# A hybrid decoder step on one core: r tiles 3 to 6 and two gate tiles as seven products of quarters, parked attention outputs, rooms chosen by time

## The chip, the cores and the metric

The kernel runs on one core of a Trainium2 chip. The metric is the device time of one execution in microseconds (us). A core has engines that run beside each other, each through its own instructions in order: TensorE for matrix products (PE in the profile, with its weight loads as PEld), VectorE (DVE), ScalarE (ACT), GpSimd (POOL) and SyncE (SP), which here issues most DMAs. Products land in PSUM, in banks of 512 fp32 numbers for each of the 128 partitions; everything else lies in SBUF.

## The reference

One layer of a decoder for 512 prompt tokens, 16 meta tokens ahead of them and 32 new tokens (8 running sequences of 4), all in fp32:

```python
h = x + 0.5 * rms_norm(swiglu(rms_norm(x, ffn1_pre_g), ...), ffn1_post_g)   # d_model 1024, d_ff 2816
u = rms_norm(h, mix_pre_g)
q_a, k_a, v_a, gk_low, r_a, q_b, k_b, v_b, gate_a, gate_b = split(u @ w_in)
o_a = gla(q_a, k_a, v_a, log_sigmoid(gk_low @ w_gk2 + b_gk) / 16)           # gated linear attention, 4 heads
o_a = rms_norm(o_a, gla_norm_g) * silu(r_a)
o_b = stick_breaking_attention(q_b, keys, values, sb_bias)                  # 16 heads; 256 cached rows for the running ones
m = sigmoid(gate_a) * (o_a @ w_o_gla) + sigmoid(gate_b) * (o_b @ w_o_sb)
h = h + rms_norm(m @ w_out, mix_post_g)
y = h + 0.5 * rms_norm(swiglu(rms_norm(h, ffn2_pre_g), ...), ffn2_post_g)
```

r_a, gate_a and gate_b are 1024 wide: eight tiles of 128 columns each. They are called r tiles, a tiles and b tiles below; "o tiles" are the eight tiles of `o_a @ w_o_gla`, "p tiles" those of `o_b @ w_o_sb`.

## The kernel before

Activations stand transposed (features on the partitions, up to 560 tokens along the row). Each fp32 factor is cut into a rounded part `hi` and a remainder `lo`, and a product is made of three: hi·hi, hi·lo and lo·hi. A tile of 128 output columns is made by `tile_steps`: eight **steps**, one for each 128 rows of the contraction, of six matmuls each (two halves of the tokens, 280 and 264 wide, by three products). `later(n, f)` puts `f` off by n steps; `when(n, f)` and `then(n, f)` put it at a step of a stage. The order of PE, DVE, ACT and GpSimd is the order in which these calls are made; SP's order is left to the framework.

**Seven products.** Two neighbouring tiles can be made together by `seven_steps`: the token columns, the contraction and the output columns are each cut in two, and seven products of quarters (272 wide, four matrix rows of blocks each) replace eight. That takes 14 steps of six matmuls instead of 16. It needs sums of quarters of the weights (`weight_sums`, four DVE operations for each pair), their hi and lo parts (`parts_of` on ACT, `parted_lo` on DVE, four of each), and sums of quarters of u. The latter are made once (`u_sums`), parked in DRAM (`sums_dram`), and read back later (`sums_back`, `sums_hi`, `sums_lo`). The seven products end in four PSUM banks, which five additions on DVE and three copies or activations on ACT put together.

**The stages.** FFN 1; the heads of linear attention, whose outputs `oa` stay in SBUF; eight attention pairs (`Pair`, 24 steps each, "pair 1" to "pair 8" being `pr` 0 to 7); then `pr` 8, in which the last pair's work ends beside r tiles 0 to 2 (24 steps); then the **mixer**, whose order is the list `MIXER`: "R" is a tile by `tile_steps`, "S" a pair by seven products. Before, that is r 3 to 7, o 0 to 7, a 0 and a 1 as R, then seven S pairs (b 0, a 2, b 2, a 4, b 4, a 6, b 6) with the p tiles between them. The first three S pairs stand side by side. After the mixer come `w_out` and FFN 2. Beside the r and o tiles, PE also does the running sequences' attention over the cache: `sample_keys` turns pages of keys (L2118), `sample_products` (L2132) gives logits, `sample_values` (L2218) weighs pages of values. Pages are gathered from DRAM by DMAs of GpSimd (L2069), into rooms that pass round in a list, `ring`.

**Weights** come by `fetch` (L186, or L621 for an S pair), into a ring of three buffers `raw`; a fetch waits until the oldest is free, that is until its `lo` part is made. An S pair's second buffer is asked for when the pair before it has made its first `lo`, five steps ahead of that pair's start, and is first read by `weight_sums` ten steps ahead of its own.

**Rooms.** SBUF tiles of varying life are taken from `Arena`: 150 units of 280 numbers, before in 25 rooms of six units. A room whose type changes (float32 or its rounded form) becomes a new tile, and its first writer waits for every earlier use of the room. `take` prefers the room that was given back longest ago, counted in gives.

## Time and profile before

| what | value |
|---|---|
| median of 3 runs | 1506.17 us (1505.92 to 1508.09) |
| profiled execution | 1508.72 us; span from first to last instruction 1507.0 us |
| granted TensorE clock | 0.999 |
| PE busy, weight loads busy | 1494.2 us, 1442.1 us |
| DVE busy, ACT busy, POOL busy | 1090.0 us, 771.5 us, 149.3 us |
| DMA | 180.40 MB, mean 120 GB/s |

The profiled execution lies 2.55 us above the median, 1.7 us of its time outside the span. Matmuls are pipelined, so the duration of one in the profile is longer than the time until the next one starts; what PE costs is read from starts.

### The profile page before, as it was taken

What the parts mean: (1) busy time and instruction counts of PE and PEld (TensorE: products, weight loads), DVE (VectorE), ACT (ScalarE), POOL (GpSimd) and SP (SyncE); (2) the same over time, 40 slices, a digit from 0 to 9 for tenths busy, and PEclk for the clock granted to TensorE, in tenths of its full rate; (3) what the DMA queues carried; (4) which work ended last, traced back from release to release, by engine and by line L of the source; (5) the groups of instructions that cost most, each with busy time, mean ns of one, the idle gap of its engine ahead of it and who ended that gap; (6) DMA issues with size and microseconds to landing.
All of it is one profiled execution on the core that took longest, in us unless ns stands there. A gap on an engine that the chain in (4) does not pass through costs nothing.

```text
span 1507.0 us, 29698 instructions
## 1 busy us (share of the span) xinstructions
PE 1494.2 (99%) x11941; PEld 1442.1 (96%) x11941; DVE 1090.0 (72%) x1939; ACT 771.5 (51%) x1422; POOL 149.3 (10%) x216
## 2 busy tenths in 40 slices
PE   9999999999999999999999999999999999999998
PEld 8999999999999889999888899999999999999998
DVE  5888888853787866877776534977567898888544
ACT  6545454533655556565555343634564555455334
POOL 2000000000000011123324551000000000000000
PEclk9999999999999999999999999999999999999999
DMA  8123333336565473335555568335532233333352
GB/s 250 55 86 99 99 98 97 88 101 195 147 160 148 122 112 85 91 82 118 131 105 139 169 204 192 105 96 144 152 103 79 85 111 99 99 99 89 86 168 98
DMA packets 276458, 180.40 MB, mean 120 GB/s; under 512 B 10154, under 2 KB 260736, under 8 KB 276320
## 3 DMA queue, kind: packets, MB, share of 16 engines
q1 hardware_dynamic: 270864, 161.64, 40.6%
q0 software_dynamic: 5440, 16.85, 3.2%
q8 instruction: 94, 1.54, 0.4%
q14 instruction: 44, 0.36, 0.1%
q10 hardware_dynamic: 16, 0.00, 0.0%
HBM read 155.72 MB, written 22.74 MB: 118 GB/s over the span
## 4 chain that ended last, share of the span: by engine, by line
PE 94%; DVE 2%; DMA 2%; ACT 1%; issue 0%; DVEq 0%; SPq 0%; ACTq 0%
PE acc L682 8%; PE acc L1248 8%; PE acc L1249 8%; PE acc L685 8%; PE acc L683 8%; PE acc L1250 8%; PE acc L695 7%; PE acc L698 7%; PE acc L696 7%; PE acc L1191 2%; PE acc L1188 2%; PE acc L1189 2%; PE acc L1028 1%; PE acc L1029 1%; PE acc L1030 1%; PE ps L2023 1%
## 5 line engine op out<-in xcount | busy, mean ns | idle before, releaser
L153 DVE TENSOR_TENSOR lo<-raw,hi 128x1024 fp32r<-128x1024 f32 (+1 forms) x213 | 254.9, 1197 | 125.9 <-ACT hi L661 102.5
L153 DVE TENSOR_TENSOR room<-room,room 128x544 f32<-128x544 f32 (+17 forms) x413 | 259.0, 649 | 81.4 <-ACT room L740 15.0
L682 PE MATMUL acc<-room,hi 128*128 128x280 f32 (+1 forms) x928 | 271.2, 309 | 0.2 <-DVE room L156 0.2
L1249 PE MATMUL acc<-room,hi 128*128 128x280 f32 (+1 forms) x896 | 259.3, 289 | 0.0
L1248 PE MATMUL acc<-room,hi 128*128 128x280 f32 (+1 forms) x896 | 259.3, 289 | 0.0
L1250 PE MATMUL acc<-room,lo 128*128 128x280 f32 (+1 forms) x896 | 259.1, 289 | 0.0
L683 PE MATMUL acc<-room,hi 128*128 128x280 f32 (+1 forms) x928 | 250.3, 289 | 0.1
L685 PE MATMUL acc<-room,lo 128*128 128x280 f32 (+1 forms) x928 | 192.8, 289 | 0.0
L682 PEld LDWEIGHTS acc<-room,hi 128*128 128x128 f32 x928 | 174.7, 188 | 13.1 <-issue 11.0
L683 PEld LDWEIGHTS acc<-room,hi 128*128 128x128 f32 x928 | 175.0, 189 | 2.8 <-issue 1.9
L1248 PEld LDWEIGHTS acc<-room,hi 128*128 128x128 f32 x896 | 168.6, 188 | 0.0
L1250 PEld LDWEIGHTS acc<-room,lo 128*128 128x128 f32 x896 | 168.6, 188 | 0.0
L1249 PEld LDWEIGHTS acc<-room,hi 128*128 128x128 f32 x896 | 168.4, 188 | 0.0
L959 ACT CAST hi<-raw 128x1024 fp32r<-128x1024 f32 x92 | 96.4, 1052 | 133.1 <-PE acc L1249 48.8
L661 ACT CAST hi<-raw 128x1024 fp32r<-128x1024 f32 (+1 forms) x121 | 122.7, 1015 | 72.0 <-DMA raw<-in_ffn_w_down_dram 18.6
L685 PEld LDWEIGHTS acc<-room,lo 128*128 128x128 f32 x928 | 145.0, 188 | 0.0
L695 PE MATMUL acc<-room,hi 128*128 128x280 f32 (+2 forms) x498 | 143.7, 296 | 0.9 <-ACT hi L661 0.9
L696 PE MATMUL acc<-room,hi 128*128 128x280 f32 (+2 forms) x498 | 141.5, 292 | 0.0
L698 PE MATMUL acc<-room,lo 128*128 128x280 f32 (+2 forms) x498 | 128.4, 292 | 0.7 <-DVE lo L153 0.7
L959 ACT CAST hi<-room 128x1024 fp32r<-128x1024 f32 x84 | 70.2, 836 | 80.8 <-PE acc L1249 60.3
L695 PE MATMUL acc<-room,room 128*128 128x280 f32 (+3 forms) x366 | 107.8, 295 | 0.0
L153 DVE TENSOR_TENSOR lo<-room,hi 128x1024 fp32r<-128x1024 f32 x84 | 80.2, 955 | 36.7 <-ACT hi L959 36.5
(406 smaller groups left out, 3299.5 us busy)
## 6 DMA issues: line engine op xcount, KB each, us to landing
raw<-in_w_in_dram SPq DMA_DIRECT2D x49, 512.0 KB
raw<-in_ffn_w_down_dram SPq DMA_DIRECT2D x40, 448.0 KB
raw<-in_ffn_w_gate_dram SPq DMA_DIRECT2D x64, 256.0 KB
raw<-in_ffn_w_up_dram SPq DMA_DIRECT2D x64, 256.0 KB
out_dram<-room SPq DMA_DIRECT2D x36, 256.0 KB
raw<-in_ffn_w_down_dram SPq DMA_DIRECT2D x14, 512.0 KB
raw<-in_w_in_dram SPq DMA_DIRECT2D x28, 256.0 KB
h_dram<-room SPq DMA_DIRECT2D x24, 280.0 KB
```

The costliest lines, as they stand in the source:

```text
L153: (eng or V).tensor_tensor(out=out, in0=a, in1=b, op=op)
L661: S.copy(h_, src)
L682: T.matmul(acc[h][:, : wid[h]], hi[k], a[h][0], start=(k == 0), stop=False)
L683: T.matmul(acc[h][:, : wid[h]], hi[k], a[h][1], start=False, stop=False)
L685: T.matmul(acc[h][:, : wid[h]], lo[k], a[h][0], start=False, stop=(k == KD - 1))
L695: T.matmul(acc[h][:nw, : wid[h]], wh, a[h][0], start=(k == 0), stop=False)
L696: T.matmul(acc[h][:nw, : wid[h]], wh, a[h][1], start=False, stop=False)
L698: T.matmul(acc[h][:nw, : wid[h]], wl, a[h][0], start=False, stop=(k == kt - 1))
L959: S.copy(hi[:, :kt], src)
L1248: T.matmul(x[:, :QW], hi, act[k][0], start=(first and k == 0), stop=False, skip_group_check=True)
L1249: T.matmul(x[:, :QW], hi, act[k][1], start=False, stop=False, skip_group_check=True)
L1250: T.matmul(x[:, :QW], lo, act[k][0], start=False, stop=(k == 3), skip_group_check=True)
```

## The change

- r tiles 3 and 4, 5 and 6, and a tiles 0 and 1 become S pairs. r 7 moves ahead of r 3. The a and b pairs stand between o tiles and p tiles in another order. The mixer's list now begins in `pr` 8.
- The sums of u are read back from pair 6 on (`SUMS_BACK` counts steps from the end of `pr` 8) instead of during the o tiles, and stay in SBUF from there.
- The outputs of linear attention are written to DRAM when they are made (`oa_dram`), given back, and read again by `oa_back` beside their r tile.
- The second halves of four of u's tiles are given back after r 7 (`halved`).
- Pages take rooms from the arena one by one, with no ring; the last three of the asks for value pages come 16 steps later.
- `Arena`: 20 rooms of six units and 15 of two; `take` compares times in steps, avoids what was given back within 12 steps, and opens an empty long room for a small tile only when others are worse.
- Sixteen small copies of the samples' outputs go from DVE to ACT; the first o tile reads its eight inputs in another order.

The diff, cut:

```diff
-KEEP = 5
-SUMS_BACK = (80, 88, 96, 104)
-MIXER = [("R", "r", n) for n in range(3, 8)]
-MIXER += [("R", "o", n) for n in range(8)] + [("R", "a", 0), ("R", "a", 1), ("S", "b", 0), ("S", "a", 2), ("S", "b", 2), ("R", "p", 0), ("R", "p", 1)]
-MIXER += [("S", "a", 4), ("R", "p", 2), ("R", "p", 3), ("S", "b", 4), ("S", "a", 6), ("R", "p", 4), ("R", "p", 5), ("S", "b", 6)]
-MIXER += [("R", "p", 6), ("R", "p", 7)]
+SUMS_BACK = (-85, -61, -37, -20)
+MIXER = [("R", "r", 0), ("R", "r", 1), ("R", "r", 2), ("R", "r", 7), ("S", "r", 3), ("S", "r", 5)]
+MIXER += [("R", "o", n) for n in range(4)] + [("S", "a", 0), ("R", "o", 4), ("R", "o", 5), ("S", "a", 2), ("R", "o", 6), ("R", "o", 7)]
+MIXER += [("S", "b", 0), ("S", "a", 4), ("R", "p", 0), ("R", "p", 1), ("S", "b", 2), ("R", "p", 2), ("R", "p", 3), ("S", "a", 6), ("S", "b", 4)]
+MIXER += [("R", "p", 4), ("R", "p", 5), ("S", "b", 6), ("R", "p", 6), ("R", "p", 7)]
-SPREAD = 15
-UNITS = 150
+UNITS, LONGS = 150, 20
...
-                since = max(f) if not empty else max(free) + SPREAD
+                other = empty and self.tile[c] is not None and self.tile[c].dtype != dt
+                since = max(free) if other else max(f)
                 waste = k % 2 == 0 and s % 2
                 alone = k == 1 and free[s ^ 1] is not None
-                key = (empty and empties <= self.keep, waste, tight and sum(x is not None for x in free), alone, since)
+                opens = empty and long and k <= self.SHORT
+                key = (opens and spare <= self.RESERVE, waste, self.now - since < self.RECENT, opens, alone, since)
...
+                for e in range(2):
+                    later(1, lambda e=e: nc.sync.dma_start(oa_dram[2 * hd + e], oa[hd, e]))
+                    later(6, lambda e=e: give(oa.pop((hd, e))))
...
-    def tile_steps(act, w1):
+    def tile_steps(act, w1, order=range(KD)):
...
     def page(src, i, c):
-        t = ring.pop(0)
+        t = take(512)
...
-                V.tensor_copy(ob[pr][r_, NP : NP + NS].rearrange("p (b t) -> p b t", t=4),
+                S.copy(ob[pr][r_, NP : NP + NS].rearrange("p (b t) -> p b t", t=4),
...
+    def oa_back(n):
+        o = take(NW)
+        nc.sync.dma_start(o, oa_dram[n])
+        return o
...
+    def r_pair(n):
+
+        o, t, sg, outs = {}, {}, {}, {}
+        q0, q1 = slice(0, QW), slice(QW, NW)
+
+        def load():
+            for i in range(2):
+                o[i] = oa_back(n + i)
+
+        def second():
+            t[1] = take(NW)
+            outs.update(c12=t[1][:, q0], c22=t[1][:, q1])
+
+        def first():
+            t[0] = take(NW)
+            outs.update(c11=lambda a: S.copy(t[0][:, q0], a), c21=t[0][:, q1])
+
+        def by_t(i):
+            sg[i] = take(NW)
+            S.activation(sg[i], t[i], AF.Sigmoid)
+            tt(o[i], o[i], t[i], ALU.mult)
+
+        def by_sg(i):
+            tt(o[i], o[i], sg[i], ALU.mult)
+            give(t[i], sg[i])
+            split(oas, n + i, o[i], oap)
+
+        for d, f in ((6, load), (10, second), (11, first), (14, lambda: by_t(1)), (15, lambda: by_sg(1)), (16, lambda: by_t(0)),
+                     (17, lambda: by_sg(0))):
+            later(d, f)
+        yield from seven_steps(("r", n), usum, QW, outs)
...
     def out_a(n):
-        acc = yield from tile_steps(oas, W1)
+        acc = yield from tile_steps(oas, W1, (0, 1, 2, 7, 3, 4, 6, 5) if n == 0 else range(KD))
...
+            if kind == "S":
+                weights_at(when, n, (what, t))
+            elif i > 1:
+                when(n - 5, st.split)
+                when(n - 4, st.fetch)
+            n += 14 if kind == "S" else 8
...
+            for m in range(2):
+                when(SUMS_BACK[i] + 6 + 4 * m, sums_hi, i, m)
+                when(SUMS_BACK[i] + 8 + 4 * m, sums_lo, i, m)
...
+        when(starts["r", 3], halved)
...
-            when(starts["b", 0] + 2 + 4 * i, lambda i=i: split(obs, i, ob[i], obp))
+            when(118 + 4 * i, lambda i=i: split(obs, i, ob[i], obp))
...
-            when(starts["a", 0] + 2 + i, ob_back, i)
+            when(102 + i, ob_back, i)
```

In the new list r 3 starts at step 8 of the mixer, r 5 at 22, o 0 at 36, a 0 at 68, b 0 at 128 and a 4 at 142; the mixer ends at step 276, before at 282.

More of the change, by code (lines that the diff above doesn't have):

```diff
@@ L69, in take @@
         best = None
-        empties = sum(None not in f for f in self.freed)
+        spare = sum(None not in f for f in self.freed if len(f) == self.LONG)
         for c, free in enumerate(self.freed):
-            empty = None not in free
+            empty, long = None not in free, len(free) == self.LONG
             if not empty and self.tile[c].dtype != dt:
                 continue
-            for s in range(self.CHUNK - k + 1):
+            for s in range(len(free) - k + 1):
                 f = free[s : s + k]
@@ L1444, in hybrid_step @@
     st.todo += [(win, 0, KD, c + P * pr, P, False) for pr in range(8) for c in (C_QB, C_KB, C_VB)]
-    st.todo += [(win, 0, KD, C_RA + P * n, P, False) for n in range(8)]
     def gate_weights(c):
@@ L2415, in hybrid_step @@
                 then(23, now.scan, 0, 3)
-            for n in FE:
+            for n in FE if now else ():
                 then(n, st.split, 0)
@@ L2445, in hybrid_step @@
                 then(SUM[1], last.meta_summed)
-            if pr == 4:
-                ring += [take(512) for _ in range(4)]
             if pr > 4:
@@ L2496, in hybrid_step @@
                 when(8 * i + 1, use_values, c, b0)
-            when(8 * i + 7, ask)
+        for i in range(3, 12):
+            when(8 * i - 17 if i < 8 else 8 * i - 1, ask)
         w1 = Weights(1)
```

136 lines of the change are left out of this document (64 added, 72 removed).

## The prediction

> **What bounds the kernel now.** First the page: its span, the busy line, and the sliced line of PE, DVE and the granted clock.
>
> ```profile
> span 1507.0 us, 29698 instructions
> PE 1494.2 (99%) x11941; PEld 1442.1 (96%) x11941; DVE 1090.0 (72%) x1939; ACT 771.5 (51%) x1422; POOL 149.3 (10%) x216
> PE   9999999999999999999999999999999999999998
> DVE  5888888853787866877776534977567898888544
> PEclk9999999999999999999999999999999999999999
> ```
>
> PE has work in every slice, at full clock; DVE is the second engine, and the slices with 3 and 4 (from 20 on) are the r and o tiles. A busy PE need not be a full one, so next the list of waits of PE (engine, line, waited for: us in total, times, longest).
>
> ```profile
> PE ps L2218 <- issue: 2.7, 5, 0.8
> PE acc L1476 <- DVE own L256: 1.1, 1, 1.1
> PE acc L695 <- ACT hi L661: 0.9, 1, 0.9
> ...
> PE ps L855 <- DVE room L153: 0.2, 1, 0.2
> ```
>
> The ten rows of the list come to 7.3 us in 1507. So the time is the number of matmuls times their spacing, and a change is worth what it takes off PE's stream, less the waits that it makes. For the spacing I read the timeline of PE in the mixer (start, duration, what).
>
> ```profile
> 949.75 0.29 PE L1028 MATMUL acc<-room,hi 128*128 128x272 f32 x1
> ...
> 960.58 0.29 PE L1028 MATMUL acc<-room,hi 128*128 128x272 f32 x1
> ...
> 970.05 0.40 PE L1028 MATMUL acc<-room,hi 128*128 128x272 f32 x1 [0.28 <-DVE room L153]
> ...
> 971.66 0.29 PE L1028 MATMUL acc<-room,hi 128*128 128x272 f32 x1
> ...
> 982.20 0.29 PE L682 MATMUL acc<-room,hi 128*128 128x280 f32 x1
> ...
> 994.27 0.29 PE L1028 MATMUL acc<-room,hi 128*128 128x272 f32 x1
> 994.40 0.29 PE L1029 MATMUL acc<-room,hi 128*128 128x272 f32 x1
> ...
> 1004.82 0.29 PE L682 MATMUL acc<-room,hi 128*128 128x280 f32 x1
> ```
>
> p 0 and p 1, two R tiles, run from 982.20 to 994.27: 12.07 us. The S pair behind them runs to 1004.82: 10.55 us. The three S pairs ahead (949.75, 960.58, 971.66, 982.20) took 10.83, 11.08 and 10.54 us: 0.81 us of loss together, in the first two.
>
> **PE's stream.** Three pairs of tiles (r 3 and 4, r 5 and 6, a 0 and 1) turn from R into S. Each saves 12.07 - 10.55 = 1.52 us, together 4.56 us: twelve matmuls of 96 in each pair, 36 in all. All other PE work stays, the samples' turns and products included; it is only moved against the tiles. This is the whole gain that I can count.
>
> [...]
>
> **DVE in the r tiles.** An S pair asks more of DVE than two R tiles. The rows by shape, from the mixer's stretch 949 to 1072, and the engines' busy time by stretch (us, then PE, PEld, DVE, ACT, POOL busy, clock, DMA share, GB/s):
>
> ```profile
> L153 DVE TENSOR_TENSOR lo<-raw,hi 128x1024 fp32r<-128x1024 f32 x21 | 25.6, 1221 | 3.9 <-ACT hi L661 3.0 <-ACT hi L959 0.6
> L153 DVE TENSOR_TENSOR room<-room,acc 128x272 f32<-128x272 f32 x28 | 11.9, 434 | 10.3 <-PE acc L1030 10.3
> L153 DVE TENSOR_TENSOR room<-room,room 128x544 fp32r<-128x544 f32 x15 | 10.8, 719 | 2.2 <-ACT room L2519 2.2
> L153 DVE TENSOR_TENSOR room<-room,room 128x544 f32<-128x544 f32 x12 | 8.4, 720 | 0.1
> L153 DVE TENSOR_TENSOR room<-raw,raw 128x512 f32<-128x512 f32 x12 | 8.3, 688 | 0.5 <-DMA raw<-in_w_in_dram 0.4
> L153 DVE TENSOR_TENSOR room<-acc,room 128x280 f32<-128x280 f32 x7 | 3.1, 450 | 7.7 <-PE acc L685 7.6
> ```
>
> ```profile
> 707.00:738.00 31.00, 31.00 (x244) 27.77 (x243) 22.91 (x52) 18.11 (x36) 10.61 (x12) 1.00 0.42 112
> 829.78:874.00 44.22, 42.91 (x415) 40.20 (x414) 21.73 (x51) 16.94 (x31) 24.45 (x25) 1.00 0.55 169
> 949.70:960.50 10.80, 10.77 (x86) 10.55 (x85) 10.61 (x20) 6.93 (x12) 0.00 (x0) 1.00 0.28 77
> 960.50:971.60 11.10, 10.82 (x86) 10.60 (x86) 10.45 (x17) 7.89 (x13) 0.00 (x0) 1.00 0.38 96
> 994.20:1004.80 10.60, 10.60 (x86) 10.60 (x86) 6.96 (x11) 4.90 (x8) 0.00 (x0) 1.00 0.26 64
> ```
>
> An r pair: 4 sums of weights at 0.69, lo parts 3 at 1.22 and one at 0.69, 5 additions at 0.43, 4 products at 0.72, 2 lo parts of the result at 0.72: 13.6 us. An r tile as R: 1.22, two reads of the bank at up to 0.45, a product and a lo part at 0.72: 3.6 us. Two pairs for four tiles: 27.2 - 14.2 = 13.0 us more. The stretch 829.78 to 874, r 3 to r 7 and what lies beside them, holds 21.73 us of DVE in 44.22; it becomes 34.7 us in 44.2 - 4 x 0.754 = 41.2 us, 84% (0.754 us is a step, 12.07 / 16). The rows put that between the pair at 10.61 of 10.80 (98%, 0.28 lost) and the one at 6.96 of 10.60 (66%, nothing lost). So DVE still fits, with its slack mostly used.
>
> What gets late first is the second of two S pairs side by side. The chain of waits shows it in the run of three (start, us, what):
>
> ```profile
> 957.50 1.42 DVE room L153 x3
> 958.99 0.98 issue
> 959.97 0.45 DVE room L153
> 960.50 8.01 DMA raw<-in_w_in_dram
> ...
> 969.21 0.79 DVE room L153 x2
> 970.05 0.40 PE acc L1028
> ```
>
> The second weight buffer took 8.01 us from there; it is asked for five steps ahead of one pair and first read ten steps ahead of the next, nine steps or 9 x 0.754 = 6.8 us apart; DVE then hands the last part over 0.28 us late, at 970.05. The new list has such neighbours at r 3/r 5, b 0/a 4 and a 6/b 4. The first has the samples' PE work between ask and read, which gives the DMA time, but more DVE work; the second is like 949.75 to 971.66. I take 0.81 us again, as before, and bounds of 0 to 3 x 0.53 = 1.6 us (0.53 being 11.08 - 10.55): net 0, from -0.8 to +0.8.
>
> **The parked outputs.** Eight writes and eight reads of 272 KB: 4.4 MB, in stretches whose DMA share is 0.42 (707 to 738) to 0.55 (829.78 to 874). The writes are covered by the attention pairs. A read for an R tile has ten steps. For an r pair it is asked at step 6 and multiplied at 14: 8 x 0.754 = 6.0 us, and DVE stands still if it is later, with the next pair's lo parts queued behind. At the 8.01 us of the row above it would be 2.0 us late; but that was a fetch that an S pair's sums waited for, and PE's sample work stretches the eight steps. I take 0, bounds 0 and 2 x 2.0 = 4.0 us.
>
> The last input of o 0, tile 5, is read seven steps into that tile: behind the end of r 5 stand an addition, a sigmoid, two products, a hi and a lo, on DVE 0.43 + 3 x 0.72 = 2.6 us, and for the two on ACT I estimate DVE's 0.72 each: 4.0 us against 7 x 0.754 = 5.3 us. It holds with 1.3 us to spare; the new order of the inputs puts the late ones last.
>
> **Sums of u.** Eight lo parts at 0.72 on DVE and eight hi parts on ACT move from the o tiles to steps 17 to 23 of pairs 6 to 8 and steps 10 to 16 of `pr` 8: 1.4 us of DVE in each, where 707 to 738 shows 22.91 busy of 31. They stand behind the turns of the weights for PE (steps 9 to 14), so 8 us of idle DVE hides them: 0, and 1.4 us for each of four stages if not.
>
> **Rooms, pages, copies.** The sums hold 32 of 150 units earlier than before, growing by 8 a pair; the parked outputs free 16, the ring up to 24. Rooms matter by waits of a first writer on the last reader. PE's listed waits leave under 2 us of these to win; what a worse choice would cost no row shows, and I bound it with the rival below. The pages were held up by their ring:
>
> ```profile
> L2069 POOL DMA_INDIRECT room<-in_cache_v_dram,idx x32: 942/946/1954, 813.9 to 920.4; - x32
> ...
>   PE ps L2118: 17.0, 5
>   PE ps L2218: 16.7, 3
> ```
>
> With rooms of their own the gathers start earlier; what then ends last is the landing. PE's 2.7 us at L2218 may go or stay; I take that they stay. The copies moved to ACT cost nothing there.
>
> **Sum.** -4.56 us on PE, 0 for the rest, with ends of -8.1 and about +4. The profiled execution would go from 1508.72 to 1504.2 us, span from 1507.0 to 1502.4; the median, 2.55 us lower, from 1506.17 to 1501.6.
>
> **Rivals.** *A, waits go too:* the 2.7 us at L2218 and the 0.81 us of the three neighbours vanish: 4.56 + 3.5 = 8.1 us, 1498.1. For it speaks that no three S pairs stand together any more and that the ring is gone; against it that the waits at L2218 are short and many, not like a late page.
>
> *B, late transfers:* all three neighbours lose 0.53 and one read of an r pair comes 2.0 us late: 0.8 + 2.0 = 2.8 us of the gain, 1504.4, no measurable difference.
>
> *C, DVE becomes the bound in the r pairs, slower than before.* DVE's waits in 829 to 874:
>
> ```profile
> DVE room L2138 <- remote: 7.0, 1, 7.0
> ...
> DVE room L153 <- PE ps L2218: 3.9, 1, 3.9
> ```
>
> The 7.0 and 3.9 us are waits in order for the samples' products on PE. If they stay, DVE needs 34.7 + 10.9 = 45.6 us in 41.2 and hands the pairs' parts over 4.4 us late; if the two reads are late as well, 4.0 us more: 8.4 - 4.56 = +3.8 us, 1510.0. It decides where the backlog passes the distance from a pair's last lo part (step 6) to its use (step 12), 6 x 0.754 = 4.5 us. Against it: a DVE that lags no longer waits for PE, so these waits shrink first.
>
> *D, a matmul is worth its duration:* 36 at 0.29 us is 10.4 us, 1495.8. Against it stand the starts 0.13 us apart. [...]
>
> **How the numbers follow.** Forecast 0.55 (1500.5 to 1503.2), A 0.14, B 0.14, C 0.15, D 0.02. A measurement tells about 0.2%, 3.0 us, from no change: the line lies at 1503.2. Faster: the forecast, less 0.01 for its edge, with A and D, 0.70. Same: B and that edge, 0.15. Slower: C, 0.15. The range goes from A's 1498.0 to 1506.0, which takes in B and the part of C's way that ends without a loss, and leaves out C's time and D, 0.17.
>
> **What would show it.** Right: 36 fewer matmuls; the three lines of the S pairs' matmuls up by 84 each; S pairs of 10.55 us from start to start; DVE at 80 to 88% in the two r pairs, and no wait of PE over 0.6 us there. Wrong: PE waiting for DVE rooms in the r pairs (C), or for `hi` at the first matmul of o 0; DVE waiting for `oa_dram` (B); new waits of PE outside the mixer, which would be the rooms' doing.

## The result, and the profile after

The kernel after took 1513.59 us (median of 5 runs, 1511.91 to 1514.8), the kernel before 1506.69 us beside it (1505.92 to 1508.09): ratio 1.0045, interval 1.0034 to 1.0057. It is slower by 6.9 us where the prediction had it 4.6 us faster. A later run of the same kernel after, beside a kernel before that took 4.0 us less (told below as e17), took 1498.96 us against 1502.73, ratio 0.9975 (0.9965 to 0.9984). Both results stand; the experiments show a part of what lies between them.

The page of the kernel after, its profiled execution (1511.91 us):

```profile
span 1509.7 us, 29753 instructions
PE 1491.4 (99%) x11905; PEld 1438.0 (95%) x11905; DVE 1103.9 (73%) x1952; ACT 783.4 (52%) x1447; POOL 143.3 (9%) x216
```

The matmuls are 36 fewer, 11905 for 11941, as counted. The groups by line (busy us, mean ns, idle before them and what ended it) show the S pairs' lines up by 84 and the R tiles' lines down by 96 each:

```profile
L686 PE MATMUL acc<-room,hi 128*128 128x280 f32 x832 | 245.1, 311 | 0.5 <-issue 0.3 <-DVE room L156 0.2
L1033 PE MATMUL acc<-room,hi 128*128 128x272 f32 x280 | 82.1, 293 | 1.2 <-issue 1.2
L1034 PE MATMUL acc<-room,hi 128*128 128x272 f32 x280 | 80.8, 289 | 0.7 <-issue 0.7
L1035 PE MATMUL acc<-room,lo 128*128 128x272 f32 x280 | 80.9, 289 | 2.0 <-issue 2.0
```

New are the idle times on the right, nearly all of them "issue": TensorE waits for nothing that the profile shows. (L686, L1033 to L1035 and L2220 of after are L682, L1028 to L1030 and L2218 of before; L2071 issues the gathers.) The timeline of PE in pair a0, where the first of the last four value pages is used (start, duration, what, idle before and its releaser) shows them one by one:

```profile
913.31 1.35 PE L2220 MATMUL ps<-room,room 128*32 128x128 f32 x23
914.98 0.27 PE L2220 MATMUL ps<-room,room 128*32 128x128 f32 x1 [0.33 <-issue]
915.72 0.38 PE L2220 MATMUL ps<-room,room 128*32 128x128 f32 x3 [0.47 <-issue]
917.11 0.41 PE L2220 MATMUL ps<-room,room 128*32 128x128 f32 x3 [1.00 <-issue]
...
919.96 0.39 PE L1035 MATMUL acc<-room,lo 128*128 128x272 f32 x1 [0.68 <-issue]
920.69 0.58 PE L1033 MATMUL acc<-room,hi 128*128 128x272 f32 x1 [0.34 <-issue]
...
922.09 0.39 PE L1035 MATMUL acc<-room,lo 128*128 128x272 f32 x1 [0.60 <-issue]
```

A value page is used in 32 short matmuls, each with its own weight load; such a run of short matmuls is called a **burst** below. The first 23 of this one run at 0.06 us each. Then TensorE's instructions, matmuls and weight loads together, come in groups of one to seven, and the groups start 0.70 to 0.73 us apart or twice that (914.98, 915.69, 917.11, 917.83, 918.54 and so on), also for the plain matmuls behind: 29 instructions from 914.98 to 922.79, 3.7 per us. The windows of the same stretch (stretch, length, PE, PEld, DVE, ACT, POOL busy with counts, granted clock, DMA share, GB/s):

```profile
905.00:912.00 7.00, 7.00 (x68) 6.55 (x67) 5.92 (x26) 1.97 (x3) 4.10 (x4) 1.00 0.54 162
912.00:918.00 6.00, 3.79 (x42) 2.24 (x41) 0.44 (x1) 1.06 (x2) 4.47 (x6) 1.00 0.64 190
918.00:921.00 3.00, 1.54 (x6) 0.92 (x6) 0.00 (x0) 0.00 (x0) 2.24 (x3) 0.76 0.56 171
921.00:925.00 4.00, 2.70 (x10) 2.19 (x10) 0.53 (x2) 0.06 (x1) 0.95 (x1) 0.50 0.74 276
```

GpSimd's gathers from 905 to 925 (operation, count, duration least/median/most in ns, first and last start):

```profile
L2071 POOL DMA_INDIRECT room<-in_cache_v_dram,idx x12: 946/949/1330, 907.0 to 921.2; - x12
```

Beside twelve gathers in one row TensorE falls to 3.79 busy us in 6, then 1.54 in 3, and behind that the granted clock falls to 0.50: at 0.50 the matmuls from 924.85 to 926.21 start 0.22 to 0.24 us apart, at full clock, from 926.41 on, 0.12 to 0.14. DVE is nearly idle too, and none of TensorE's waits in this stretch names it.

Before, the last four gathers came behind this burst, since the first of them waited for the burst's own matmuls (L2218). After, the first of the twelve waits for an operation of DVE (L2206) and the others hardly at all (0.30 or 0.31 us each). That gather before and after (start, duration, what, idle before and its releaser):

```profile
916.16 0.95 POOL L2069 DMA_INDIRECT room<-in_cache_v_dram,idx  x1 [13.96 <-PE ps L2218]
```

```profile
906.98 1.33 POOL L2071 DMA_INDIRECT room<-in_cache_v_dram,idx  x1 [6.87 <-DVE room L2206]
```

The account, from the start of each mixer step in the two traces: the mixer begins 2.8 us earlier (in a later run of the kernel before's own code, e4, it began 2.1 earlier too, so most of this is no effect of the change); steps 0 and 1 lose 2.1; steps 17 to 20, in pair r 3, lose 3.1; before's own losses at three bursts, 2.1 and twice 1.06, are gone, -4.2; steps 80 to 83, in a0 and o4, lose 9.5; from step 139 to the mixer's end the new list takes 5.3 less, 4.5 for six steps fewer (three pairs of 14 for 16) and 0.8 for neighbouring pairs that lose nothing any more. Small drifts make -0.4 inside the mixer and +0.7 behind it. Together +2.7, by which the spans differ. In the list of waits of PE (us in total, times, longest), asked for the stretches 828 to 833, 849 to 854 and 912 to 925, they are:

```profile
PE ps L2191 <- DVE room L153: 1.4, 1, 1.4
...
PE acc L1033 <- issue: 0.8, 1, 0.8
PE acc L1035 <- issue: 0.8, 1, 0.8
PE acc L1034 <- issue: 0.7, 1, 0.7
...
PE ps L2220 <- issue: 2.6, 5, 1.0
PE acc L1035 <- issue: 1.3, 2, 0.7
```

### The profile page after: what moved, and what is told of

It is laid out like the page before. It is cut to its first block, busy times and chain, and to the rows that moved or that the text cites. A ratio compares the mean times of both kernels' runs of the same rounds, so it can differ in the third digit from the quotient of the medians.

```text
span 1509.7 us, 29753 instructions
## 1 busy us (share of the span) xinstructions
PE 1491.4 (99%) x11905; PEld 1438.0 (95%) x11905; DVE 1103.9 (73%) x1952; ACT 783.4 (52%) x1447; POOL 143.3 (9%) x216
## 3 DMA queue, kind: packets, MB, share of 16 engines
q8 instruction: 93, 1.52, 0.4%
## 4 chain that ended last, share of the span: by engine, by line
PE 93%; DVE 3%; ACT 1%; issue 1%; DMA 1%; SPq 0%; DVEq 0%; ACTq 0%
PE acc L1253 8%; PE acc L1254 8%; PE acc L1255 8%; PE acc L686 7%; PE acc L687 7%; PE acc L689 7%; PE acc L699 7%; PE acc L702 6%; PE acc L700 6%; PE acc L1033 2%; PE acc L1035 2%; PE acc L1034 2%; DVE room L153 2%; PE acc L1196 1%; PE acc L1194 1%; PE acc L1193 1%
## 5 line engine op out<-in xcount | busy, mean ns | idle before, releaser
L153 DVE TENSOR_TENSOR room<-room,room 128x544 fp32r<-128x544 f32 (+17 forms) x427 | 265.0, 644 | 58.8 <-ACT room L745 12.6
L1253 PE MATMUL acc<-room,hi 128*128 128x280 f32 (+1 forms) x896 | 259.5, 290 | 0.0
L1254 PE MATMUL acc<-room,hi 128*128 128x280 f32 (+1 forms) x896 | 259.4, 290 | 0.0
L1255 PE MATMUL acc<-room,lo 128*128 128x280 f32 (+1 forms) x896 | 259.3, 289 | 0.0
L686 PE MATMUL acc<-room,hi 128*128 128x280 f32 x832 | 245.1, 311 | 0.5 <-issue 0.3
L687 PE MATMUL acc<-room,hi 128*128 128x280 f32 x832 | 225.7, 290 | 0.4 <-issue 0.4
L964 ACT CAST hi<-raw 128x1024 fp32r<-128x1024 f32 x98 | 103.0, 1056 | 142.9 <-PE acc L1254 73.0
L689 PE MATMUL acc<-room,lo 128*128 128x280 f32 x832 | 173.5, 290 | 0.5 <-DVE lo L153 0.5
L686 PEld LDWEIGHTS acc<-room,hi 128*128 128x128 f32 x832 | 157.2, 189 | 13.4 <-issue 11.4
L1255 PEld LDWEIGHTS acc<-room,lo 128*128 128x128 f32 x896 | 168.8, 188 | 0.0
L1253 PEld LDWEIGHTS acc<-room,hi 128*128 128x128 f32 x896 | 168.5, 188 | 0.0
L1254 PEld LDWEIGHTS acc<-room,hi 128*128 128x128 f32 x896 | 168.5, 188 | 0.0
L687 PEld LDWEIGHTS acc<-room,hi 128*128 128x128 f32 x832 | 157.6, 189 | 2.8 <-issue 1.9
L665 ACT CAST hi<-raw 128x1024 fp32r<-128x1024 f32 (+1 forms) x115 | 116.6, 1015 | 80.1 <-issue 22.4
L689 PEld LDWEIGHTS acc<-room,lo 128*128 128x128 f32 x832 | 130.6, 189 | 1.1 <-DVE lo L153 0.7
L153 DVE TENSOR_TENSOR room<-room,acc 128x272 f32<-128x272 f32 (+1 forms) x176 | 74.3, 437 | 57.2 <-PE acc L1255 19.2
```

Source lines behind the costliest of these rows:

```text
L153: (eng or V).tensor_tensor(out=out, in0=a, in1=b, op=op)
L665: S.copy(h_, src)
L686: T.matmul(acc[h][:, : wid[h]], hi[k], a[h][0], start=(k == order[0]), stop=False)
L687: T.matmul(acc[h][:, : wid[h]], hi[k], a[h][1], start=False, stop=False)
L689: T.matmul(acc[h][:, : wid[h]], lo[k], a[h][0], start=False, stop=(k == order[-1]))
L964: S.copy(hi[:, :kt], src)
```

## The experiments

**Theories.** *Supply:* TensorE lacks no data; it receives its instructions too slowly while GpSimd issues a **row** of gathers (one behind the other, about 1.25 us from start to start) and TensorE wants many short instructions at once, and behind the idling its granted clock falls (0.50 from 919.5 to 926.4 in after). The change moved the gathers: before asked for the last value pages at steps 47, 55, 63 and 87, after at 63, 71, 79 and 87. *Late pages:* the pages land late. *r pairs:* rival C, DVE too slow. The runs are labelled e1 to e18 in their order. All runs of one group below shared a chip and the runs of the kernel before. Steps are counted from 0 at the mixer's start. The loss of a step in a run's trace is read against the same step of e17, which has no such idle time (e4 against before), and stands for one execution. The changes to the code are shown shortened.

**First group: the gathers (before 1506.65).** What is fetched, how, and when:

```diff
 e1:  t = take(512)                      # last three value pages only
-     G.indirect_dma_start(out=t, ...)
+     G.memset(t, 1.0)
 e2:
+     nc.sync.dma_start(t, src[P * i : P * i + P])
 e3:  when(60, filler)                   # 64 x T.matmul of 32x32 by 32
 e4:  # kernel before
-     when(8 * i + 7, ask)
+     when(8 * i - 17 if i < 8 else 8 * i - 1, ask)
```

> The kernel after, with the twelve gathers of the last three value pages left out: their buffers are taken at the same place and filled with ones by GpSimd (so part of the sample output is not computed from the cache). The first of the last four pages, which TensorE uses at the place of the 9.5 us loss, is still gathered. Supply theory (TensorE waits for no data there, but receives its instructions slowly while the gathers of later pages are issued and their transfers load the DMA queues): the 9.5 us at mixer steps 80 to 83 go, 1513.6 - 9.5 = 1504.1 us, and no half clock is left in the mixer. Late-page theory (the first page lands late): it is fetched as before, so 1513.6. Theory of the r pairs (rival C of the prediction, DVE too slow): 1513.6.

Measured 1504.53 us (1501.61 to 1505.95), ratio 0.9983 (0.9974 to 0.9993): 9.1 us faster than after. The first page, which TensorE uses at 912, was still gathered, and in the profiled execution (1501.61 us, the fastest of the ten) the stretch that had lost 9.5 us is full at full clock:

```profile
912.00:918.00 6.00, 6.00 (x73) 5.65 (x72) 3.35 (x6) 2.03 (x3) 0.00 (x0) 1.00 0.33 84
918.00:921.00 3.00, 3.00 (x50) 2.73 (x48) 2.70 (x5) 0.00 (x0) 0.00 (x0) 1.00 0.60 169
```

Late pages and r pairs fall as causes of the large loss. The 3.1 us of steps 17 to 20, beside other gathers (nine from 838.9 to 851.4 in after), stayed. TensorE has plain matmuls there, with four short transposes ahead of them and no burst.

> The kernel after, with the twelve gathers of the last three value pages replaced by ordinary transfers of the same size from fixed rows of the cache, issued by SyncE (so the page table is not followed for them). It splits the supply theory: if GpSimd's issuing of the gathers is what slows TensorE's instructions, the loss at steps 80 to 83 goes, about 1504; if it is the bytes in flight, it stays, 1511 to 1516. Late-page theory and r-pair theory: 1513.6 (unless SyncE's queue holds other loads back, which would show as waits for weights).

Measured 1502.2 us (1501.63 to 1506.11), ratio 0.9974 (0.9963 to 0.9985). It is not the bytes in flight: with the same data moved by SyncE's transfers the DMA share is higher than in after, 0.95 for 0.64, and TensorE is full.

```profile
912.00:918.00 6.00, 6.00 (x73) 5.65 (x72) 2.12 (x5) 1.67 (x4) 0.00 (x0) 1.00 0.95 327
```

> The kernel after, with 64 further matmuls of 32x32 by 32 columns on TensorE at mixer step 60, ahead of the loss, into a PSUM buffer that nobody reads. [...] The matmuls themselves cost 1 to 3 us. [...] In the form that gathers beside a burst suffice: the loss stays, 1514.6 to 1516.6. Late-page and r-pair theories: 1514.6 to 1516.6.

Measured 1521.81 us (1519.6 to 1524.11), ratio 1.0104 (1.0087 to 1.0121), outside the 1514.6 to 1516.6 that stands above for supply, where gathers beside a burst suffice, and for its rivals alike. The added matmuls were not the 1 to 3 us that I gave them: their own step took 7.0 us more, and the half clock behind it 2.0 more on the next three. The old loss stands at steps 86 to 89 (5.3 us) instead of 80 to 83. That does not show that it matters by how many instructions the later ones are shifted: in e8, whose code ahead of step 170 is that of after, 7.6 us are lost at steps 86 to 90 and nothing at 80 to 83. The run has 256 instructions more (30009 for 29753), four for each added matmul of the program. The page of after lists 93 packets and 1.52 MB for queue 8, "instruction", 16 KB each, and the 23810 records of TensorE make 256 for each of them. If that queue carries TensorE's instructions, which no run shows, the shift is one whole packet; whether a packet's border has a part in the loss stays open.

> The kernel before, with one part of the change alone: its page gathers are asked for at the steps of the kernel after (63, 71, 79, 87 in place of 47, 55, 63, 87). Supply theory: gathers now stand beside the first burst of the last values, so the loss comes with them, 1506.7 + 5 to 10 = 1512 to 1517. If the rooms' new choice or the r pairs are the cause instead, nothing comes: 1506.2 to 1507.2. Late-page theory: each page is still asked for 18 steps of 0.75 us before its use, so nothing: 1506.7.

Measured 1514.07 us (1513.91 to 1515.01), ratio 1.0049 (1.0032 to 1.0066): +7.4 us, as supply expected. With nothing but the later asks the kernel before becomes as slow as the kernel after. The loss came at another burst, the short matmuls of the second half's new keys at step 65, beside a row of eight gathers. The waits of PE from 895 to 907, the gathers from 890 to 905, and two windows:

```profile
PE ps L2165 <- issue: 4.5, 7, 1.2
```

```profile
L2069 POOL DMA_INDIRECT room<-in_cache_v_dram,idx x8: 949/949/955, 893.0 to 901.8; - x8
```

```profile
900.00:904.00 4.00, 0.96 (x12) 0.68 (x13) 0.00 (x0) 0.00 (x0) 2.17 (x3) 0.89 0.70 227
904.00:907.00 3.00, 2.62 (x28) 2.54 (x28) 1.62 (x6) 2.04 (x5) 0.00 (x0) 0.50 0.17 56
```

**Second group: other steps for the same gathers (before 1507.32).**

```diff
 e5, e6:
-        for i in range(3, 12):
-            when(8 * i - 17 if i < 8 else 8 * i - 1, ask)
+        for n in (7, 15, 23, 31, 39, 55, 73, 83, 91):      # e5
+        for n in (7, 21, 25, 31, 39, 55, 73, 83, 91):      # e6
+            when(n, ask)
 e6, e7:
-                then(17, lambda: todo.extend([n, f] for n, f in w0.pieces(1)))
+                then(15, lambda: todo.extend([n, f] for n, f in w0.pieces(1)))
```

> The kernel after with only the last four asks for value pages moved, from steps 63, 71, 79, 87 to 55, 73, 83, 91; all is computed as in the reference. Supply theory: fewer gathers stand in one row ahead of the burst at step 81, so the 9.5 us there shrink to 0 to 2, in all 1503.5 to 1507. If it is the number of gathers in a row whatever the steps say (GpSimd runs ahead of TensorE and issues them as soon as their buffers are free), the row only moves: 1508 to 1516. Theory of the r pairs: nothing, 1513.6.

Measured 1511.69 us, ratio 1.0029 (1.0019 to 1.0038); the runs spread from 1506.33 to 1513.8. The row only moved: GpSimd did not keep step with TensorE, and ten gathers from 907.8 to 920.8 still stood in one row. That is the second alternative. The profiled execution, at 1506.33 the fastest of the ten, loses only 3.2 us beside this row, at steps 84 to 87: a row does not cost the same each time.

> As the run before, and two asks of the r pairs moved (from steps 15, 23 to 21, 25) and the sample's first weights begun two steps earlier, so that the turn at step 1 does not fall behind the sums of r3 on DVE. All is computed as in the reference. Supply theory: besides the 9.5 us, the 3.1 us at steps 17 to 20 go, and 2.1 us at steps 0 and 1 by the wait for DVE: 1513.6 - 9.5 - 3.1 - 2.1 = 1498.9, range 1498.5 to 1503. Theory that the rows of gathers only move: 1504 to 1514. Theory of the r pairs: only the 2.1 go, 1511.5.

Measured 1505.1 us (1500.84 to 1506.52), ratio 0.998 (0.9969 to 0.9991): better, but in the range of the alternative. In its trace the 2.1 us of steps 0 and 1 are gone (now 0.5 less than before), the 3.1 of steps 17 to 20 too, and 2.0 us are lost at step 80. But 3.2 at steps 24 to 30, 1.1 at 40 and 0.7 at 65 are new.

> The kernel after with one edit: the sample's first weights are begun two steps earlier, so that their turn on TensorE (steps 0 and 1, 2.1 us lost against the kernel before, 1.4 of it a wait for DVE) comes ahead of r3's sums on DVE. If that wait is the order on DVE: 1513.6 - 2.1 = 1511.5. If DVE's whole load there is the bound (rival C), it comes back a few steps later: 1513.6.

Measured 1510.88 us (1506.71 to 1515.0), ratio 1.0031 (1.0019 to 1.0044), 2.7 below after. The list of waits of PE from 825 to 834 is empty; the turn (a transpose on PE) had only stood behind r 3's sums on DVE. The order was at fault and not DVE's load, since nothing of it comes back as a wait for DVE. Its profiled execution, the fastest of the six, loses its large part, 5.6 us, at steps 86 to 88 and not at 80 to 83: at plain matmuls beside the row, from 918.1 on, some 4 us behind the burst.

**Third group: rows of gathers (before 1507.02).**

```diff
 e8, e9:
+    ts = [take(512) for _ in range(4)]       # when(170, ...)
+    for j in range(32):
+        G.indirect_dma_start(out=ts[j % 4], ...)
+    later(60, lambda: give(*ts))
 e9:  when(182, filler)
 e10, e11:  # Arena.take, for the last four pages
+                if fresh:
+                    key = (other, waste, alone, opens, -since)
 e10: asks at 7, 21, 25, 31, 39, 63, 74, 83, 91; weights begun at 15
 e11: asks at 7, 21, 25, 31, 39, 57, 73, 83, 91; weights begun at 15
```

> The kernel after, with 32 further gathers of cache rows issued back to back by GpSimd at mixer step 170, far behind the last burst, into four buffers that nobody reads. It asks whether a row of gathers alone starves TensorE, without a burst of short matmuls. 32 gathers of 1.25 us make 40 us. In the gaps of after TensorE got 8 instructions per 0.70 us, 11.4 per us; its plain matmuls with their weight loads want 2 per 0.126 us, 15.9 per us. If the slow supply holds for all gathers, 40 x (15.9 - 11.4) = 180 instructions are missing, up to 180 / 15.9 = 11 us less what stands ready: 3 to 11 us lost near there, and gaps of 0.7 us. If a burst must use up the stock first: 0 to 1 us lost. Late-page and r-pair theories: 0, since nobody reads these rows.

Measured 1536.57 us (two runs), ratio 1.0196 (1.0176 to 1.0217), for a reason that none of the theories had: my buffers. They were handed on to the loads of h, which wait on SyncE for the last gather, and the next weights stood behind them in that queue. In the chain of waits (start, us, what) the last gather's landing, the h load, the weights:

```profile
1023.43 3.65 DMA room<-in_cache_v_dram,idx
...
1027.09 0.34 SPq L2617
...
1029.09 5.08 DMA raw<-in_w_in_dram
```

And the wait that came of it, in the list of waits of PE:

```profile
PE acc L1033 <- DVE room L153: 18.9, 1, 18.9
```

Up to that stop, at step 201, the run still answers its question. In the window from 977 to 1018 stand 24 gathers and no burst, and TensorE loses nothing:

```profile
977.00:1018.00 41.00, 41.00 (x329) 40.87 (x328) 22.51 (x34) 13.11 (x20) 26.83 (x24) 1.00 0.65 208
```

> As the run before, and 64 further matmuls of 32x32 by 32 columns (with 64 weight loads) on TensorE at mixer step 182, beside the further gathers, into a buffer that nobody reads. Supply theory: 128 more instructions are wanted inside the row of gathers, so over the run before 1.8 us for the matmuls themselves and 5 to 9 us of gaps of 0.7 us come, with a stretch of half clock. If the loss in after had to do with its own pages or with the sample's work: 1.8 us and no gaps.

Measured 1538.11 us (two runs), ratio 1.0207 (1.0178 to 1.0235). The two totals cannot be set against each other, since the trace of e9 has no stop of 18.9 us. The steps can: steps 187 to 191, which lose nothing in e8 beside the same gathers, lose 14.0 us in e9, six microseconds behind the added burst, with eleven idle times of TensorE of up to 1.5 us from 1015 to 1031 and a mean granted clock of 0.58 from 1020 to 1040. So on this chip the row of gathers made no gap by itself, and with a burst it did. I repeated the pair on e10, which has few losses of its own (e12 to e14).

> The kernel after with its first weights begun two steps earlier and two asks of the r pairs at 21 and 25 as in the version of the asks and weights moved, the last four asks at 63, 74, 83, 91, and the buffers of the last four pages chosen among those given back last instead of longest ago, so that GpSimd, which waits for a buffer's last reader, cannot run ahead of TensorE with all twelve gathers in one row. All is computed as in the reference. Supply theory (the length of the row decides): no loss over 2 us is left at steps 80 to 90, 1499 to 1503. If the sum of gathers decides whatever their spacing: 1504 to 1510. Late-page theory: pages land later now, so waits for them come at steps 81 to 105, 1506 to 1515.

Measured 1499.89 us (1499.19 to 1501.69), ratio 0.9956 (0.9939 to 0.9973): 7.1 us faster than the kernel before and 13.7 faster than after on chips of this kind. Where GpSimd had to wait for a buffer's last reader (from 885 to 925 once 15.6 us for PE and twice 3.0 for DVE), the row broke up: four gathers from 904.8, a pause at 909 to 913 in which the burst falls, then eight. The burst's window is full at full clock; 2.2 us are still lost at steps 19 to 31. The buffers are not all that differs from after: against e6, which has the earlier weights and the same two asks of the r pairs, e10 is 5.2 us faster.

```profile
905.00:912.00 7.00, 7.00 (x91) 6.30 (x90) 3.37 (x10) 2.10 (x3) 4.26 (x4) 1.00 0.66 194
```

> As the run before, with the first of the last four asks at step 57 and the second at 73 instead of 63 and 74: 1499 to 1503 by the supply theory, with a difference of under 2 us to the run before. If the first burst at step 81 starves wherever eight gathers stand ahead of it in the last 16 steps, this one, with one page earlier, is the faster by 2 to 5.

Measured 1502.62 us (1500.14 to 1504.03), ratio 0.9965 (0.9951 to 0.9979). By the medians it is the slower of the two by 2.7 us, over the 2 us that supply gave, though the runs overlap, and not the faster by 2 to 5: no sign that eight gathers ahead of the burst at 81 decide. Neither trace loses anything at steps 80 to 90; that of e11, its slowest run, loses 3.4 us at steps 94 to 96.

**Fourth to sixth group: gathers and burst apart, on the base of e10 (before 1507.27 for e12 and e13, 1502.33 for e14).**

```diff
 e12: 16 gathers as in e8, when(170, ...)
 e13: the same, and when(158, filler)
 e14: when(158, filler) alone
```

> The version with fresh buffers (1499.9 us, its own stalls gone), with 16 further gathers issued back to back by GpSimd behind the last burst (asked for at mixer step 170), into four buffers that nobody reads and that are given back well before SyncE wants them. Supply theory in the form that a burst must first use up what stands ready for TensorE: no gap of 0.7 us beside these gathers, 1499.5 to 1501.5. In the form that gathers alone slow TensorE's instructions: 16 x 1.25 = 20 us at 15.9 - 11.4 = 4.5 missing instructions per us, up to 6 us, 1502 to 1506.

Measured 1503.11 us (1501.89 to 1505.24), ratio 0.9972 (0.9962 to 0.9981): 3.2 us over e10, more than the 1.5 expected, but the trace has no instruction gap beside these gathers; its one idle stretch, 1.35 us at 997.5, is a wait for DVE. The r pairs and the tiles up to step 40, far ahead of the added gathers, lose 2.7 us more than in the trace of e10.

> As the run before, with 64 matmuls of 32x32 by 32 columns and their 64 weight loads on TensorE at mixer step 158, in the midst of those gathers, into a buffer that nobody reads; nothing here waits for data. Supply theory: 1.8 us for the matmuls and a stall of 3 to 10 us in groups of 7 to 8 instructions per 0.7 us that ends 1 to 3 us after the last gather: 1504 to 1511. If bursts are harmless and the loss in after had another cause: 1.8 us, 1501.5 to 1503.

Measured 1512.83 us (1508.39 to 1515.06), ratio 1.0033 (1.0024 to 1.0043), 9.7 over e12. Taken alone it looks like the supply theory's number. The timeline has gaps in the burst, but only three, and they end 14 us before the last gather (L2582 is the added burst):

```profile
978.42 3.70 PE L2582 MATMUL ps<-ones 32*32 32x32 f32 x111
982.54 0.42 PE L2582 MATMUL ps<-ones 32*32 32x32 f32 x5 [0.43 <-issue]
983.30 0.46 PE L2582 MATMUL ps<-ones 32*32 32x32 f32 x5 [0.34 <-issue]
984.06 0.56 PE L2582 MATMUL ps<-ones 32*32 32x32 f32 x7 [0.30 <-issue]
```

> The control of the run with 16 gathers and a burst: the version with fresh buffers and the same 64 matmuls (128 matmul records, since each f32 matmul is two passes) at mixer step 158, without the further gathers. In the run with gathers 111 of these records started in 3.70 us, so 128 without a gap take 4.3 us. Theory that burst and gathers are both needed: 1499.9 + 4.3 = 1504.2 us, 1503.5 to 1505.5, no gap over 0.5 us in the burst and no half clock behind it. Theory that a burst alone outruns TensorE's instructions: the gaps and the half clock of the run with gathers come here too, 1508 to 1513.

Measured 1505.5 us (1501.65 to 1506.22) against 1502.33, ratio 1.0013 (1.0004 to 1.0023). Without a gather beside it the burst's step cost 5.05 us (6.22 in e13), with no idle time listed among its 128 records, and the half clock came all the same, 2.0 us more on the next three steps as in e13. That is the profiled execution, the slowest of the ten (mean granted clock 0.996); the fastest, 1501.65 us, had 1.0, so the half clock did not come each time. Windows of e14:

```profile
973.00:978.00 5.00, 5.00 (x129) 4.85 (x129) 3.82 (x5) 1.79 (x2) 0.00 (x0) 0.82 0.56 129
978.00:981.00 3.00, 3.00 (x19) 2.94 (x17) 0.69 (x1) 0.00 (x0) 0.00 (x0) 0.50 0.17 50
```

So 7.0 of the 8.2 us that e13 loses at these steps also come without gathers. Whether the gathers add the other 1.2 is not shown, since the two runs had different chips. The added burst was a poor copy of the kernel's own. And e14 showed something larger: on its chip the kernel before took 1502.33 us, and the trace had none of the gaps in the r pairs that the earlier versions of the kernel after had shown.

**Seventh and eighth group: the kernel's own burst laid out thinly, and the chip (before 1502.58 and 1502.73).**

```diff
 e15, e16, e18:   # value pages of c = 1; e15, e18 on after, e16 on e10
-                when(8 * i + 1, use_values, c, b0)
+                for part in range(4 if c else 1):
+                    when(8 * i + 1 - (3 - part if c else 0), use_values, c, b0, part, ...)
 e17: the kernel after, unchanged
```

> The kernel after with one edit: each of the last four value pages is used in four parts on four successive mixer steps (78 to 81, 86 to 89 and so on, 8 matmul records each) instead of 32 records at once on the last of them. Gathers, buffers, the order of all else and the number of TensorE instructions stay, and all is computed as in the reference. If the loss of 9.5 us needs the burst (the instructions wanted at once, while gathers are issued): 1504 to 1508. If only the number of instructions wanted over the whole row of gathers counts, or the burst does not matter: 1511 to 1516. Late-page theory: the page is wanted three steps (2.3 us) earlier, 1513 to 1518.

Measured 1502.95 us (1502.43 to 1504.74), ratio 1.0005 (0.9995 to 1.0014). The number is the first theory's; the reason was not, since the gaps of steps 17 to 20, which this edit does not touch, were missing as well.

> The version with fresh buffers (0.9956 of the time before) with the same spreading of the last four value pages over four steps each; all is computed as in the reference. Its traces show no gap at these steps any more, so spreading should bring nothing where the row of gathers is already cut up: ratio 0.995 to 0.997. If the spread bursts cost (more switches of the matmuls' shape): 0.997 to 0.999.

Measured 1500.56 us (1499.54 to 1501.35), ratio 0.9988 (0.9978 to 0.9997). The ratio cannot be set against e10's 0.9956, whose kernel before was 4.4 us slower; but the steps that carry the parts take about 1.0 us more for each page, 4 us in all: spreading costs.

> The kernel after, unchanged, beside the run with the spread burst on one chip. On the chips of the last three runs the kernel before took 1502.3 to 1502.6 us and not 1506.2 to 1507.3, and no gap of 0.7 us stood in their traces even where the kernel after had lost 3.1 us (steps 17 to 20). So the spread burst has to be compared on the same chip. If before takes 1506 to 1508 here (a chip with the gaps): after 1511.5 to 1515, as in its first runs. If before takes 1502 to 1503 here: by the theory that the gaps are a matter of the single chip as well, after loses its gaps too and keeps the saving of the S pairs, the wait at steps 0 and 1: 1500 to 1505; if the gaps of the last value pages come on every chip: 1509 to 1512.

Measured 1498.96 us (1498.03 to 1499.86) against 1502.73, ratio 0.9975 (0.9965 to 0.9984): on this chip the change makes the kernel faster. The row of gathers stands beside the burst as in the first trace of after, with as many bytes in flight, and TensorE has no gap. The gathers of e17, and its windows:

```profile
L2071 POOL DMA_INDIRECT room<-in_cache_v_dram,idx x12: 942/946/1723, 904.5 to 919.7; - x12
```

```profile
905.00:912.00 7.00, 7.00 (x90) 6.30 (x89) 3.88 (x14) 2.10 (x3) 5.48 (x6) 1.00 0.71 209
912.00:918.00 6.00, 6.00 (x48) 5.86 (x47) 4.90 (x7) 1.38 (x2) 4.78 (x5) 1.00 0.59 163
918.00:921.00 3.00, 3.00 (x49) 2.80 (x48) 0.10 (x2) 1.06 (x3) 2.01 (x3) 1.00 0.93 323
```

Against the first trace of the same kernel, r 3 takes 14.87 us for 17.98 and a0 with o4 20.47 for 30.09: 12.7 us, and the spans differ by 12.2.

> The spread burst again, beside the kernel after on the same chip. If before takes 1506 to 1508 here: 1505 to 1509 where the burst is needed for the 9.5 us, within 2 us of after where it is not. If before takes 1502 to 1503 here: 1502.5 to 1504, after plus 0 to 3, since the spreading itself costs 0.56 us on each step that carries a part but takes nothing away.

Measured 1503.03 us (1502.43 to 1504.97), ratio 1.0004 (0.9995 to 1.0014), 4.1 us slower than e17 on the same chip and just over the 0 to 3 expected. Spreading the burst took nothing away in e15: on a chip of this kind the kernel after has no gaps without it.

**What follows.** Shown on chips where the kernel before takes 1506 to 1507: the gathers of the last pages are needed for the large loss (e1), as gathers and not as bytes (e2); added rows of them far from any burst made no gap (e8, e12), and such a row with a burst did (e9); moving the asks alone makes a loss of that size (e4), and in e10, where the row is broken, it is gone. At which steps beside the row the loss falls, and how large it is, differs between the executions (e5, e7, e8). Shown too: where the kernel before takes 1502.3 to 1502.7, the same instructions make no gap (e17), and the traces of e14 to e18 have none anywhere in the mixer.

Four things are open. The first is what differs between these chips: all runs of the first kind were made ahead of those of the second, and one of the 19 runs of the kernel before beside e17 took 1507.05 us, so it may not be the chip alone. The second is by what way a gather holds TensorE up: "too few instructions" is the reading of idle time with no wait in the profile, and no run shows the way. The third is what a burst without gathers does on a chip of the first kind. The fourth is whether a burst is needed: e9 speaks for it, though its gaps come 6 us later, at plain matmuls, and the gaps of steps 17 to 20 have none ahead of them.

## Why the prediction was wrong, point by point

- **-4.56 us on PE: right.** 36 fewer matmuls, and six steps fewer at 0.754 us are 4.5 of the 5.3 us gained from step 139 on. The S pairs from b 0 on run 10.52 to 10.53 us from start to start for the 10.55 forecast. Rival D's 10.4 us did not come.
- **DVE at 80 to 88% in the r pairs, and no wait of PE there: right where no gap disturbs.** The window about the two r pairs in e17 has DVE 27.40 in 33.00 us, 83% (80% in the pairs alone, 839.24 to 867.65), with PE busy throughout; rival C fell, and the list of waits of PE from 836 to 876 in e17 is empty. The sum had begun r 3 one step early: 829.78 is the last step of r 2.

```profile
836.00:869.00 33.00, 33.00 (x344) 31.42 (x344) 27.40 (x49) 18.95 (x32) 19.70 (x16) 1.00 0.89 280
```

- **Neighbouring pairs lose 0.81 us again: wrong by 0.8, in the change's favour.** b 0 and a 4 take 10.52 and 10.53, undisturbed, and so do a 6 and b 4. Of rival A this half came. The parked outputs cost nothing that a wait shows.
- **"With rooms of their own the gathers start earlier; what then ends last is the landing": this step failed.** I read the 2.7 us at L2218, all "issue", as a fixed small cost, and put the moved gathers at zero because their data would be there in time. The data were there: TensorE's waits at the loss name no DMA. But "issue" was idle time beside rows of GpSimd's gathers, and it went with where the gathers stood: moving the asks alone cost 7.4 us (e4), and after lost 9.5 us at steps 80 to 83. The range's upper end, 1506.0, held nothing for it, since I had bounded the move by waits for data alone.
- **Gathers that "start earlier": wrong in direction as well.** The twelve of the last pages that stand beside the burst were issued from 907.0 to 921.2; before, the step of the burst ran from 914.4 to 916.2 and the last four came only behind it, up to 920.4. The later asks, and rooms that no longer wait for the burst, put them into one row.
- **The half clock: missing in the sum.** The trace has 0.50 for some 6.8 us (919.5 to 926.4), in which plain matmuls that follow one another start 0.22 to 0.24 us apart where 0.12 to 0.14 is usual, so the loss here was more than the idle times.
- **The turn at steps 0 and 1: 2.1 us on PE, put at zero.** r 3's sums of weights stand ahead of it on DVE. I had weighed DVE's load and not the order on its queue; begun two steps earlier, it is gone (e7).
- **Rooms: a small gain or loss, in bounds, as far as waits go.** Behind the mixer the trace of after takes 0.7 us more, that of e4 0.4 more, so little of it is theirs. Inside it they decided when a gather was issued (the waits of 13.96 and 6.87 us above), and that the sum left out.

Where the gaps do not occur, the forecast was near: -3.8 us measured for -4.6, with the 2.1 us lost and 0.8 won in between, so a part of the nearness is luck. The count of matmuls and the load of DVE were right. What decided was a cost that the trace of before already carried, as three small losses of 4.2 us together, and that I took for constant. The 4.2 us are about what the kernel before takes less on the second kind of chip (1506.7 to 1507.3 against 1502.3 to 1502.7); no trace of it was kept there, so that these are the same losses is an estimate.

## What to carry to other kernels

Waits put down to "issue" in a burst of short matmuls were a warning here (2.7 us before, and 9.5 lost at one burst after): look at what GpSimd issues beside them, and price a move of its gathers by that, not by the landing of the data alone. GpSimd, which waited only for buffers, did not keep the steps of the asks (twelve gathers in one row from 907.0 to 921.2 in after); with buffers given back last the row broke (e10, a pause at 909 to 913). With earlier weights and other asks that made 13.7 us here; the nearest pair of runs, e6 and e10, puts the buffers and two asks at 5.2 us. And a gain under 1% should be measured on several chips before it is believed or dropped: the same two kernels came out at 1.0045 at first and at 0.9975 on the chip of e17.

## What the runs showed of the hardware

- Beside a row of gathers, on chips where the kernel before took 1506.7 to 1507.3 us, TensorE's instructions came in small groups 0.70 to 0.73 us apart: 3.7 instructions per us from 914.98 to 922.79 in after, where plain matmuls with their weight loads want 2 per 0.126 us (96 in 12.07 us in the kernel before), 15.9 per us. The 11.4 per us in the expectations of e8 and e12 would need eight in every group, and the groups had one to seven. Beside 24 gathers in e8, far from any burst, there was no such gap (PE busy 41.00 of 41.00 us from 977 to 1018).
- The granted clock of TensorE was 0.50 for some 6.8 us in after (919.5 to 926.4), behind idle times that began at 914.65; the longest time from one instruction of TensorE to the next there was 1.28 us. In e14 it was 0.82 on the mean from 973 to 978 and 0.50 from 978 to 981, during and behind 128 records of 32x32 matmuls that ran 5.03 us without an idle time, while the fastest run of e14 had a mean of 1.0. What makes the clock fall is not shown.
- The kernel before took 1506.7 to 1507.3 us on some chips and 1502.3 to 1502.7 on others, with 5 to 19 runs each, within about 3 us but for the one run told above. Whether it is the chip that differs is open.
